# A hybrid encoder layer on one core: where the mixers' copies run, the output projection's priority, and the place of x's last rows

## The chip, the cores and the metric

The kernel runs on one core of one Trainium2 chip. A core has five engines that the text names: TensorE (PE; PEld is its loading of weights), VectorE (DVE), ScalarE (ACT), GpSimd (POOL) and SyncE (SP), which here issues nearly all DMAs. Data lies in SBUF; PE writes its sums to PSUM, from where VectorE or ScalarE has to copy them. The metric is the device time of one execution in microseconds (us), the median of several runs.

## The reference, cut to what matters

One inference step of one encoder layer for two groups of frames: 1024 new ones (`x_prompt`, T rows 0 to 1023) and 64 of running streams (`x_sample`, rows 1024 to 1087), width 1024.

```python
p = _rmsnorm(x, norm_mix[l]) @ w_in[l]            # all mixers' inputs, 3076 columns
conv_o, conv_h = _conv_module(cv_a, cv_g, ...)    # gate, depthwise conv of 31 taps, layer norm over 256, silu
fox_o = ...                                       # softmax attention with forget gates, blocks of 128 rows
s_fin, hg_o = lax.scan(_hgrn_chunk ...)           # gated linear recurrence in chunks of 64
sb_o = ...                                        # stick-breaking attention
mix = concat[conv_o, fox_o, hg, sb_o]             # 4 x 256 columns
x = x + mix @ w_out[l]
x = x + _mem_attend(_rmsnorm(x, norm_mem[l]), mk, mv, w_mq[l], w_mo[l])
h = _rmsnorm(x, norm_ffn[l])
return x + jnp.square(jax.nn.relu(h @ w_up[l])) @ w_down[l]
```

The last step is one more norm. Outputs are both groups' results and the new caches and states.

## The kernel before

Everything is kept transposed, features on the partitions and the 1088 rows along the free axis. A dense product in full precision is made from three: each operand is split into a high and a low part (`split`, the line of VectorE's half is L171, ScalarE's is L74), and `mm3` issues for each of the 8 blocks of the contraction two matmuls with the weights' high part (`wh`) and one with the low part (`wl`). All matmuls are recorded at L71.

The stages, in program order:

- *Start.* SP loads the nine row tiles `xt0` to `xt8` (L254). PE transposes them block by block into `px` (L282), ScalarE and VectorE scale and split `px` (L285) and copy it (`xs`, L289) to `xT_d` in DRAM; `stats` makes the rows' norms and spreads them with `dg` and `pr` over the partitions (`rb`). `xt0` to `xt6` have buffers of their own, `xt7` lies in a buffer of the tag "vn", and `xt8`, which holds `x_sample`, in the only buffer of the tag "kT". The first `kT` of the attention (the stick-breaking lane's keys, L441) therefore waits until PE has transposed all of `xt8`.
- *Mixers.* Four lanes are written as generators: projections, attention (fox and stick-breaking), convolution, HGRN. The loop at the end interleaves their steps by estimated time and gives each a priority (`tc.cur_priority`); a scheduler then lays down a fixed order for each engine, in which of the instructions that can go the one of the smallest number goes first. Projections have the smallest, then attention, HGRN, convolution and the products of the memory (PR_MM); everything that follows has PR_END, the largest. Each engine works through its order strictly; SP's DMAs too.
- *Copies.* Attention transposes its weights on PE (`pt`, L517); `evac` copies them from PSUM to `aT`, and the attention's and HGRN's results likewise (`o`, `hvn`, `hkn`, `hsc`). A counter sends each fourth copy to VectorE (L310), the others to ScalarE.
- *Convolution.* Two tiles of 128 channels (`y_4800` and `y_4816`), three chunks of rows, 31 taps each on VectorE (L794). In the last chunk the new conv cache is copied out (`cvo`, L805). Then, for either half of the chunk, PE sums over channels (`pme`), VectorE subtracts the mean (L816), ScalarE squares, PE sums again (`pva`), and the norm (L149, L152 to L154), scale and bias (L825, L826), sigmoid (ScalarE, L166) and product (L830) follow; SP stores the result to `mix_d`, slots 0 and 1 (L832 to L835). `cv` has a single PSUM buffer.
- *Output projection.* `split_mix` (L1036 and after) loads a slot of `mix_d` and splits it: slots 0 and 1 are the convolution, 2 and 3 fox, 4 and 5 HGRN, 6 and 7 stick-breaking. `dense_add(0, w_out, ...)` adds the product for group 0 (rows 0 to 511), 8 x 8 x 3 = 192 matmuls `pa` of 512 columns, and L1120 adds `pa` to x. The norm for the memory's attention follows, then `dense_add(1, ...)` for group 1 (576 rows, in 320 and 256 columns), whose order MIX takes slots 0 and 1 last. The convolution's last chunk belongs to group 1 alone.
- *After that* memory attention, the MLP up and down, and the final norm; their order is the same in both kernels.

Of the kernel before, what the change touches and what calls it, by code (L numbers as in the profile page):

```python
# [8 lines left out]
F32 = mybir.dt.float32  # L9
# [3 lines left out]
AF = mybir.ActivationFunctionType  # L13
# [4 lines left out]
P = 128  # L18
D = 1024
# [3 lines left out]
T = SP + SS  # L23
# [15 lines left out]
P_COST = 18.0  # L39
PROJ_ORDER = "sb0 h0 sb1 ff cv fox0 h1 fox1 kv".split()  # L40

PR_PROJ, PR_ATT, PR_HGRN, PR_CONV, PR_MM, PR_END = (i * 10 ** 6 for i in (1, 2, 3, 4, 5, 10))


class Need:
# [7 lines left out]
def kernel(ctx: ExitStack, tc: tile.TileContext, *args):  # L53
# [16 lines left out]
    def mm(out, lhsT, rhs, start, stop, **kw):  # L70
        nc.tensor.matmul(out, lhsT=lhsT, rhs=rhs, start=start, stop=stop, **kw)  # L71

    def act(out, in_, func, **kw):
        nc.scalar.activation(out=out, in_=in_, func=func, **kw)  # L74

    V, Q = nc.vector, nc.gpsimd
# [33 lines left out]
    for m in LEVELS[1:]:  # L110
        nb = 64 // m
        f = const.tile([P, nb], F32, name=f"lf{m}", tag="lvlf", bufs=1)
# [27 lines left out]
    def rstd_chain(pool, n, mean_sq, tag, scale=1.0, parts=P, out=None, tiles=None):  # L140

        tags = [tag + c for c in "vyt"] if isinstance(tag, str) else tag
        tags = [dict(tag=g) if isinstance(g, str) else dict(zip(("tag", "bufs"), g)) for g in tags]
        if tiles:
            v, y, t = tiles[0][:, :n], out, tiles[1][:, :n]
        else:
            v, y, t = (out if c == "y" and out is not None else pool.tile([P, n], F32, name="rs" + c, **g)[:parts]
                       for c, g in zip("vyt", tags))
        V.tensor_scalar(out=v, in0=mean_sq, scalar1=scale, scalar2=EPS, op0=ALU.mult, op1=ALU.add)  # L149
        act(y, v, AF.Ln)  # L150
        act(y, y, AF.Exp, scale=-0.5)
        V.tensor_tensor(out=t, in0=y, in1=y, op=ALU.mult)  # L152
        V.scalar_tensor_tensor(out=t, in0=t, scalar=-0.5, in1=v, op0=ALU.mult, op1=ALU.mult)
        V.scalar_tensor_tensor(out=y, in0=t, scalar=1.5, in1=y, op0=ALU.add, op1=ALU.mult)  # L154
        return y
# [21 lines left out]
    def fetch_w(src, r0, kt, c0, cols=P):  # L177
        raw = wp.tile([P, KD, P], F32, name="wr", tag="wr")[:, :kt, :cols]
        nc.sync.dma_start(out=raw, in_=src[r0:r0 + kt * P, c0:c0 + cols].rearrange("(k p) c -> p k c", p=P))
        return raw  # L180
# [60 lines left out]
    att = mx.enter_context(tc.tile_pool(name="att", bufs=2))  # L241
    wk = mx.enter_context(tc.tile_pool(name="wk", bufs=2))
    rb = wk.tile([P, T], F32, name="rb", tag="rb", bufs=1)
    with ExitStack() as pa:
        xa = pa.enter_context(tc.tile_pool(name="xa", bufs=1))
        ps_a = pa.enter_context(tc.tile_pool(name="ps_a", bufs=4, space=PSUM))
        ss = xa.tile([P, 9], F32, name="ss")
        V.memset(ss, 0.0)
        junk = att.tile([P, 2, D], BF16, name="junk", tag="vn")
        xt = []  # L250
        for i, (t0, n) in enumerate(TT):
            xt.append((att.tile([P, T], F32, name=f"xt{i}", tag=("vn", "kT")[i - 7], bufs=(2, 1)[i - 7])[:, :D] if i >= 7 else
                       xa.tile([P, D], F32, name=f"xt{i}")))
            nc.sync.dma_start(out=xt[i][:n], in_=x_prompt[t0:t0 + n] if i < 8 else x_sample)  # L254
            if i in (3, 6):
                c = (C_SK, C_SV)[i // 3 - 1]
                early[c] = fetch_w(w_in, 0, KD, c)

        def stats(c0, cn, tiles):
            for i in tiles:  # L260
                n = TT[i][1]
                if i % 2:
                    V.tensor_tensor_reduce(out=junk[:n, 1], in0=xt[i][:n], in1=xt[i][:n], scale=1.0, scalar=0.0,
                                           op0=ALU.mult, op1=ALU.add, accum_out=ss[:n, i:i + 1])
                else:
                    act(junk[:n, 0], xt[i][:n], AF.Square, accum_out=ss[:n, i:i + 1])
            r = rstd_chain(xa, len(tiles), ss[:, tiles[0]:tiles[0] + len(tiles)], "ra", scale=1.0 / D)
            pr = ps_a.tile([P, 512], F32, name="pr", tag="pr", bufs=1)
            for j, i in enumerate(tiles):
                n = TT[i][1]  # L270
                dg = xa.tile([P, P], F32, name="dg", tag="dg", bufs=2)
                V.tensor_scalar(out=dg[:n, :n], in0=ident[:n, :n], scalar1=r[:n, j:j + 1], scalar2=None, op0=ALU.mult)
                mm(pr[:, j * P:j * P + n], ones[:n], dg[:n, :n], True, True)
            act(rb[:, c0:c0 + cn], pr[:, :cn], AF.Copy)

        for c0, cn in CH:
            tiles = [i for i, (t0, n) in enumerate(TT) if c0 <= t0 < c0 + cn]
            for k in range(KD):
                px = ps_a.tile([P, 512], F32, name="px", tag="px")
                for i in tiles:  # L280
                    t0, n = TT[i]
                    nc.tensor.transpose(px[:, t0 - c0:t0 - c0 + n], xt[i][:n, k * P:(k + 1) * P], ident[:n, :n])  # L282
                hi, lo = h_at(k, c0, cn)
                act(hi, px[:, :cn], AF.Identity, scale=g_mix[:, k:k + 1])
                V.scalar_tensor_tensor(out=lo, in0=px[:, :cn], scalar=g_mix[:, k:k + 1], in1=hi.bitcast(F32),  # L285
                                       op0=ALU.mult, op1=ALU.subtract)
                xs = xa.tile([P, 512], F32, name="xs", tag="xs", bufs=4)
                if k % 2:
                    V.tensor_copy(out=xs[:, :cn], in_=px[:, :cn])  # L289
                else:  # L290
                    act(xs[:, :cn], px[:, :cn], AF.Copy)
                nc.sync.dma_start(out=xT_d[:, k, c0:c0 + cn], in_=xs[:, :cn])
            stats(c0, cn, tiles)
# [6 lines left out]
    ps_cv = mx.enter_context(tc.tile_pool(name="ps_cv", bufs=1, space=PSUM))  # L300
    hc = mx.enter_context(tc.tile_pool(name="hc", bufs=1))

    flip = [0]

    def evac(out, in_):
        flip[0] = (flip[0] + 1) % 4
        if flip[0]:
            act(out, in_, AF.Copy)
        else:
            V.tensor_copy(out=out, in_=in_)  # L310

    pending = [None, 0]

# [702 lines left out]
    while lanes:  # L1016
# [13 lines left out]
            ln.need = y.key  # L1030
        else:
            ln.t += y * ln.rate
    tc.cur_priority = PR_END

    def split_mix(k, src, t0, n, which):
        nc.sync.dma_start(out=src, in_=mix_d[k][:, t0:t0 + n])  # L1036
# [28 lines left out]
    def wide():  # L1065
        return unit("aq")
# [11 lines left out]
    def rms_stats(g, psum, tag, tiles=None, keep=False, s2=None):  # L1078

        if not s2:  # L1080
            for k in range(KD):
                s2 = add_square(g, k, s2, wide())
        rr = unit("tm")
        for c0, cn in GR[g][2]:
            ps = psum.tile([P, 512], F32, name="pr", tag=tag)
            mm(ps[:, :cn], ones, s2[:, c0:c0 + cn], True, True)
            v, t = tiles or (unit("tm"), unit("tm"))
            rstd_chain(None, cn, ps[:, :cn], "xxx", scale=1.0 / D, out=rr[:, c0:c0 + cn], tiles=(v, t))
            if keep:
                V.tensor_tensor(out=t[:, :cn], in0=v[:, :cn], in1=rr[:, c0:c0 + cn], op=ALU.mult)  # L1090
                nc.sync.dma_start(out=rms_d[:, c0:c0 + cn], in_=t[:, :cn])
        return rr
# [7 lines left out]
    def rms_apply(g, gains, rr, which, over=False):  # L1100

        dst = [pair(which) for _ in range(KD)]
        for c0, cn in GR[g][2]:
            for k in range(KD):
                hf = normed(g, k, gains, rr, c0, cn, xT[g][k] if over else None)
                split(dst[k][0][:, c0:c0 + cn], dst[k][1][:, c0:c0 + cn], hf[:, :cn])
        return dst

    def dense_add(g, src, r0, kt, a, psum, ahead=None, store=False, after=None, order=None):

        t0, n, _ = GR[g]
        for m in (0, 4, 1, 5, 2, 6, 3, 7) if after else range(KD):
            w = load_w(src, r0, kt, m * P)
            if ahead:
                ahead(m)
            for c0, cn in GR[g][2]:
                ps = psum.tile([P, 512], F32, name="pa", tag="mm")
                mm3(ps[:, :cn], w, lambda k: (a[k][0][:, c0:c0 + cn], a[k][1][:, c0:c0 + cn]), kt, order=order)
                xs = xT[g][m][:, c0:c0 + cn]
                V.tensor_tensor(out=xs, in0=xs, in1=ps[:, :cn], op=ALU.add)  # L1120
            if store:
                nc.sync.dma_start(out=x2_d[m][:, t0:t0 + n], in_=xT[g][m])
            if after:
                tc.cur_priority += 600
                after(m)
                tc.cur_priority -= 600
# [3 lines left out]
    with ExitStack() as pm_:  # L1130
# [94 lines left out]

        MIX = (2, 3, 4, 5, 6, 7, 0, 1)
        dense_add(0, w_out, 0, KD, mix[0], ps1, ahead)
        h2 = rms_apply(0, g_mem, rms_stats(0, ps2, "sc"), 0)
        dense_add(1, w_out, 0, KD, mix[1], ps1, lambda m: load_x(1, m), order=MIX)
        for g in range(2):  # L1230
# [321 lines left out]
```

## Time and profile before

| | us |
|---|---|
| median of 3 runs | 1765.38 (1765.11 to 1768.04) |
| the profiled execution | 1760.05 |
| its span, first to last instruction | 1758.3 |
| PE busy | 1694.8 (96%) |
| VectorE busy | 1172.1 (67%) |
| ScalarE busy | 791.4 (45%) |
| mean granted clock of PE | 0.991 |

The profile is one execution, recorded by the hardware profiler; times count from the first instruction. "Busy" leaves out the issuing of DMAs, and PE's matmuls are pipelined, so that their rows overlap. An idle time is put down to the instruction that released it, the one that came last. The granted clock is PE's, as a share of its full 2.4 GHz: 0.50 is its lower level of 1.2 GHz, and a window between the two has parts at either.

### The profile page before, as it was taken

The page shows a single profiled execution, that of the slowest core. Times are in us where ns is not written, and L with a number is a line of the kernel's source. Part 1 is how long each engine was busy: PE and PEld are TensorE (multiplying, and loading weights), DVE is VectorE, ACT ScalarE, POOL GpSimd, SP SyncE. Part 2 cuts the span into 40 slices and gives each one's busy share as a digit, 9 for nine tenths or more (in the row PEclk, how much of TensorE's full clock was granted, in tenths as well). Part 3 has the DMA queues.
Part 4 walks back from the last instruction along what each step waited for, and adds up shares of the span by engine and source line. Part 5 has one row for each costly group of instructions (what it writes and reads, how often), then busy time and mean ns, then how long its engine had stood idle before and what let it go on. Part 6 is the DMA issues. An engine that isn't in the chain of part 4 may idle for free.

```text
span 1758.3 us, 29395 instructions
## 1 busy us (share of the span) xinstructions
PE 1694.8 (96%) x11379; PEld 1504.8 (86%) x11379; DVE 1172.1 (67%) x2231; ACT 791.4 (45%) x1614; POOL 94.1 (5%) x201
## 2 busy tenths in 40 slices
PE   6999999999989979999999999999999999999997
PEld 4987768787777768988899989999999999999987
DVE  6266789988986897667777696555556444444435
ACT  6265657547447855346456363433334212122213
POOL 3021111101120200000000000000000000000000
PEclk9999999999999989999999999999999999999999
DMA  8521332242237348232522343333335722332112
GB/s 256 142 80 33 111 87 88 71 123 76 71 95 215 111 140 254 73 97 67 156 78 73 101 124 99 99 106 99 101 105 203 266 94 87 99 100 74 37 37 102
DMA packets 233195, 194.70 MB, mean 111 GB/s; under 512 B 17502, under 2 KB 199711, under 8 KB 233055
## 3 DMA queue, kind: packets, MB, share of 16 engines
q1 hardware_dynamic: 232639, 192.54, 35.6%
q8 instruction: 90, 1.47, 0.4%
q14 instruction: 50, 0.41, 0.1%
q10 hardware_dynamic: 160, 0.26, 0.0%
q0 software_dynamic: 256, 0.01, 0.0%
HBM read 137.96 MB, written 53.72 MB: 109 GB/s over the span
## 4 chain that ended last, share of the span: by engine, by line
PE 75%; DVE 15%; ACT 4%; DMA 3%; issue 2%; POOL 0%; SPq 0%; DVEq 0%; POOLq 0%; ACTq 0%
PE pz L71 24%; PE pw L71 15%; PE pm L71 11%; PE pa L71 9%; PE pq L71 5%; PE z L71 2%; DVE y L794 2%; PE pmo L71 2%; PE pms L71 1%; PE po L71 1%; PE pt L517 1%; PE pv L71 1%; DVE wl L171 1%; DVE hsc L934 1%; DVE sba L494 1%
## 5 line engine op out<-in xcount | busy, mean ns | idle before, releaser
L74 ACT ACTIVATE wh<-wr 128x1024 fp32r<-128x1024 f32 (+1 forms) x179 | 161.4, 909 | 439.6 <-PE pz L71 195.2
L171 DVE TENSOR_TENSOR wl<-wr,wh 128x1024 fp32r<-128x1024 f32 (+1 forms) x179 | 184.3, 1036 | 63.8 <-ACT wh L74 62.5
L71 PE MATMUL pw<-ap,wh 128*128 128x512 f32 x720 | 223.3, 391 | 1.0 <-DVE xt L1120 0.6
L71 PE MATMUL pz<-ap,wh 128*128 128x288 f32 x988 | 198.3, 294 | 0.0
L71 PE MATMUL pa<-ap,wh 128*128 128x256 f32 (+2 forms) x768 | 187.0, 332 | 2.1 <-DVE xt L1120 2.1
L71 PE MATMUL pm<-hx,wh 128*128 128x512 f32 (+1 forms) x640 | 176.6, 363 | 2.1 <-ACT wh L74 1.4
L71 PEld LDWEIGHTS pz<-ap,wh 128*128 128x128 f32 x988 | 161.3, 188 | 4.6
L71 PE MATMUL pm<-ap,wh 128*128 128x256 f32 (+1 forms) x768 | 164.7, 307 | 0.0
L71 PEld LDWEIGHTS pw<-ap,wh 128*128 128x128 f32 x720 | 130.0, 188 | 23.5 <-issue 0.8
L71 PE MATMUL pz<-ap,wl 128*128 128x288 f32 x494 | 145.4, 294 | 0.0
L71 PEld LDWEIGHTS pa<-ap,wh 128*128 128x128 f32 x768 | 132.3, 191 | 12.5 <-DVE xt L1120 2.4
L71 PE MATMUL pw<-ap,wl 128*128 128x512 f32 x360 | 140.3, 390 | 0.0
L71 PEld LDWEIGHTS pm<-hx,wh 128*128 128x128 f32 x640 | 110.2, 192 | 20.6 <-ACT wh L74 2.2
L71 PEld LDWEIGHTS pm<-ap,wh 128*128 128x128 f32 x768 | 123.8, 191 | 4.2 <-issue 1.7
L71 PE MATMUL pa<-ap,wl 128*128 128x512 f32 (+2 forms) x384 | 127.2, 332 | 0.1
L1349 DVE TENSOR_TENSOR xt<-xt,pz 128x576 f32<-128x576 f32 x56 | 42.2, 753 | 115.6 <-PE pz L71 108.8
L71 PE MATMUL pm<-ap,wl 128*128 128x256 f32 (+1 forms) x384 | 114.0, 297 | 0.0
L71 PE MATMUL pm<-hx,wl 128*128 128x512 f32 (+1 forms) x320 | 112.7, 352 | 0.1
L794 DVE SCALAR_TENSOR_TENSOR y<-ext,cwT,y 128x376 f32<-128x376 f32 (+1 forms) x180 | 100.9, 604 | 0.3
L1349 DVE TENSOR_TENSOR xt<-xt,pw 128x512 f32<-128x512 f32 (+2 forms) x80 | 51.0, 638 | 69.8 <-PE pw L71 67.6
L71 PE MATMUL pq<-ap,wh 128*128 128x512 f32 (+2 forms) x384 | 93.0, 331 | 0.0
L71 PEld LDWEIGHTS pz<-ap,wl 128*128 128x128 f32 x494 | 92.7, 188 | 0.0
(385 smaller groups left out, 3572.9 us busy)
## 6 DMA issues: line engine op xcount, KB each, us to landing
wr<-in_w_up_dram SPq DMA_DIRECT2D x32, 512.0 KB, 4.1
wr<-in_w_down_dram SPq DMA_DIRECT2D x32, 512.0 KB, 3.5
wr<-in_w_in_dram SPq DMA_DIRECT2D x24, 512.0 KB, 4.3
hid_d<-ap SPq DMA_DIRECT2D x32, 288.0 KB, 2.4
aq<-hid_d SPq DMA_DIRECT2D x32, 288.0 KB, 3.7
wr<-in_w_out_dram SPq DMA_DIRECT2D x16, 512.0 KB, 4.2
wr<-in_w_mq_dram SPq DMA_DIRECT2D x16, 512.0 KB, 3.8
wr<-in_w_mo_dram SPq DMA_DIRECT2D x32, 256.0 KB, 2.8
```

Source lines behind the costliest of these rows:

```text
L71: nc.tensor.matmul(out, lhsT=lhsT, rhs=rhs, start=start, stop=stop, **kw)
L74: nc.scalar.activation(out=out, in_=in_, func=func, **kw)
L171: V.tensor_tensor(out=lo, in0=src, in1=hi.bitcast(F32), op=ALU.subtract)
L494: V.tensor_tensor_scan(out=v[:, ::-1], data0=z[:, n - 1:0:-1], data1=v[:, ::-1], initial=-NEG, op0=ALU.add, op1=ALU.subtract)
L517: nc.tensor.transpose(ps[:w, j - jb], p[:, j * P:j * P + w], ident)
L794: V.scalar_tensor_tensor(out=y, in0=ext[:, j:j + n], scalar=cwT[:, ct, j:j + 1], in1=y, op0=ALU.mult, op1=ALU.add)
L934: V.copy_predicated(sc[r, s_at:s_at + ng, :, r].rearrange("p g h (c w) -> p (g h) c w", w=2 * m)[:, :, :, m:], lvl[m][r, par * nb:(par + 1 ...
L1349: eng.tensor_tensor(out=out, in0=a, in1=b, op=ALU.add)
```

## The change

Three edits. First, `evac` always uses ScalarE; the counter goes. 40 copies move: 11 of `aT` with 512 columns, 4 with 384, 6 with 256 and 4 with 128, 7 of `o`, and 8 of HGRN's and others. Second, a priority PR_OUT lies between HGRN and the convolution, whose number and that of the memory's products rise by one; the splits of `mix` and group 0 of the output projection get it, and what follows has PR_END as before. Third, `xt8` lies in the buffer of the tag "q2" and no longer in that of "kT". Lines after `evac` move up by five.

```diff
--- before.py
+++ after.py
@@ -39,7 +39,7 @@
 P_COST = 18.0
 PROJ_ORDER = "sb0 h0 sb1 ff cv fox0 h1 fox1 kv".split()
 
-PR_PROJ, PR_ATT, PR_HGRN, PR_CONV, PR_MM, PR_END = (i * 10 ** 6 for i in (1, 2, 3, 4, 5, 10))
+PR_PROJ, PR_ATT, PR_HGRN, PR_OUT, PR_CONV, PR_MM, PR_END = (i * 10 ** 6 for i in (1, 2, 3, 4, 5, 6, 10))
 
 
 class Need:
@@ -249,8 +249,9 @@
         junk = att.tile([P, 2, D], BF16, name="junk", tag="vn")
         xt = []
         for i, (t0, n) in enumerate(TT):
-            xt.append((att.tile([P, T], F32, name=f"xt{i}", tag=("vn", "kT")[i - 7], bufs=(2, 1)[i - 7])[:, :D] if i >= 7 else
-                       xa.tile([P, D], F32, name=f"xt{i}")))
+            xt.append(att.tile([P, T], F32, name="xt7", tag="vn")[:, :D] if i == 7 else
+                      att.tile([P, 2, T], F32, name="xt8", tag="q2", bufs=1)[:, 0, :D] if i == 8 else
+                      xa.tile([P, D], F32, name=f"xt{i}"))
             nc.sync.dma_start(out=xt[i][:n], in_=x_prompt[t0:t0 + n] if i < 8 else x_sample)
             if i in (3, 6):
                 c = (C_SK, C_SV)[i // 3 - 1]
@@ -300,14 +301,8 @@
     ps_cv = mx.enter_context(tc.tile_pool(name="ps_cv", bufs=1, space=PSUM))
     hc = mx.enter_context(tc.tile_pool(name="hc", bufs=1))
 
-    flip = [0]
-
     def evac(out, in_):
-        flip[0] = (flip[0] + 1) % 4
-        if flip[0]:
-            act(out, in_, AF.Copy)
-        else:
-            V.tensor_copy(out=out, in_=in_)
+        act(out, in_, AF.Copy)
 
     pending = [None, 0]
 
@@ -1030,7 +1025,7 @@
             ln.need = y.key
         else:
             ln.t += y * ln.rate
-    tc.cur_priority = PR_END
+    tc.cur_priority = PR_OUT
 
     def split_mix(k, src, t0, n, which):
         nc.sync.dma_start(out=src, in_=mix_d[k][:, t0:t0 + n])
@@ -1225,6 +1220,7 @@
 
         MIX = (2, 3, 4, 5, 6, 7, 0, 1)
         dense_add(0, w_out, 0, KD, mix[0], ps1, ahead)
+        tc.cur_priority = PR_END
         h2 = rms_apply(0, g_mem, rms_stats(0, ps2, "sc"), 0)
         dense_add(1, w_out, 0, KD, mix[1], ps1, lambda m: load_x(1, m), order=MIX)
         for g in range(2):
```

The three fences below show each engine's fixed order, so `x4` are four instructions in a row.

PE at the start, before: `px` are the transposes of x (`xt_240` holds `x_sample`), `pr` spreads the norms, `pn` transposes the first keys, `pm` are projection matmuls.

```order
L282 MATMUL px<-ident,xt_234 128x128
L282 MATMUL px<-ident,xt_238 128x128
L282 MATMUL px<-ident,xt_240 128x64
L71 MATMUL pr<-dg,ones 128x128
L71 MATMUL pr<-dg,ones 128x64
L482 MATMUL pc<-ident,kv 128x128
L365 MATMUL pn<-ident,kT 128x128 x4
L482 MATMUL pc<-ident,kv 128x128 x3
L71 MATMUL pm<-ap,wh 128x256 x2
```

The same place after:

```order
L283 MATMUL px<-ident,xt_238 128x128
L283 MATMUL px<-ident,xt_240 128x64
L360 MATMUL pn<-ident,kT 128x128 x4
L71 MATMUL pm<-ap,wh 128x256 x2
L71 MATMUL pm<-ap,wl 128x256
L71 MATMUL pm<-ap,wh 128x256 x2
L71 MATMUL pm<-ap,wl 128x256
L71 MATMUL pm<-ap,wh 128x256 x2
L71 MATMUL pm<-ap,wl 128x256
L71 MATMUL pm<-ap,wh 128x256 x2
L71 MATMUL pm<-ap,wl 128x256
L71 MATMUL pr<-dg,ones 128x128 x2
```

The keys' transposes and twelve projection matmuls have moved ahead of the last transposes of x.

PE where the mixers end, before: `pv` is the last attention, `pa` the output projection, `pme` and `pva` the convolution's two sums.

```order
L71 MATMUL pv<-aT,vn 64x128 x5
L71 MATMUL pa<-ap,wh 128x512 x4
L71 MATMUL pme<-y_4800,ones 128x183
L71 MATMUL pme<-y_4816,ones 128x183
L71 MATMUL pa<-ap,wl 128x512
L71 MATMUL pa<-ap,wh 128x512 x2
L71 MATMUL pa<-ap,wl 128x512
L71 MATMUL pva<-sq_5331,ones 128x183
L71 MATMUL pva<-sq_5332,ones 128x183
```

PE after, at the end of group 0:

```order
L71 MATMUL pa<-ap,wh 128x512 x2
L71 MATMUL pa<-ap,wl 128x512
L71 MATMUL pva<-sq_5332,ones 128x183
L71 MATMUL pa<-ap,wh 128x320 x2
L71 MATMUL pa<-ap,wl 128x320
```

The other sums stand among earlier matmuls `pm`; the last `pva` has moved behind all 192 `pa` of group 0.

VectorE at the end of the taps, before (the taps L794 of either tile stand 23 in a row ahead of this):

```order
L794 SCALAR_TENSOR_TENSOR y_4800<-ext_4785,cwT,y_4800 128x366
L794 SCALAR_TENSOR_TENSOR y_4816<-ext_4801,cwT,y_4816 128x366
L805 COPY cvo<-pco 30x256 x2
L171 TENSOR_TENSOR ap<-mix,ap 128x512
L171 TENSOR_TENSOR wl<-wr,wh 128x1024
L816 SCALAR_TENSOR_TENSOR y_4800<-pme,y_4800 128x183
```

The same end of the taps after:

```order
L171 TENSOR_TENSOR ap<-mix,ap 128x512
L789 SCALAR_TENSOR_TENSOR y_4800<-ext_4785,cwT,y_4800 128x366
L171 TENSOR_TENSOR ap<-mix,ap 128x512
L966 TENSOR_TENSOR ho<-htv,po 128x64
L789 SCALAR_TENSOR_TENSOR y_4816<-ext_4801,cwT,y_4816 128x366
L171 TENSOR_TENSOR wl<-wr,wh 128x1024
L789 SCALAR_TENSOR_TENSOR y_4800<-ext_4785,cwT,y_4800 128x366
```

The splits of `mix` and of the weights have moved in among the taps.

## Rows read from the trace of the kernel before

**Rows 1.** Busy line of the page: busy us, share of span, instructions

```profile
PE 1694.8 (96%) x11379; PEld 1504.8 (86%) x11379; DVE 1172.1 (67%) x2231; ACT 791.4 (45%) x1614; POOL 94.1 (5%) x201
```

**Rows 2.** What PE waits for: us in total, times, longest us

```profile
PE pme L71 <- DVE cvo L805: 9.1, 1, 9.1
...
PE z L71 <- DVE sba L494: 3.2, 4, 1.1
...
PE pt L517 <- ACT sba L74: 2.6, 6, 0.8
...
PE pd L71 <- DVE hsc L934: 2.5, 2, 2.0
...
PE pv L71 <- ACT aT L74: 1.4, 2, 0.9
```

**Rows 3.** Window: length, busy PE PEld DVE ACT POOL, PEclk, DMA share, GB/s

```profile
308.00:352.00 44.00, 41.99 (x319) 33.75 (x319) 41.61 (x75) 26.18 (x45) 6.38 (x11) 1.00 0.27 72
```

**Rows 4.** Window, line L310 alone: length, VectorE busy, then as above

```profile
0.00:720.00 720.00, 18.55 (x40) 0.98 0.42 121
```

**Rows 5.** Groups by form: busy us, mean ns, idle before, releaser

```profile
L310 DVE COPY aT<-pt 128x512 f32<-128x512 f32 x11 | 7.5, 683 | 0.2 <-PE pt L517 0.2
...
L74 ACT ACTIVATE aT<-pt 128x512 f32<-128x512 f32 x41 | 24.3, 593 | 17.6 <-PE pt L517 17.4
```

**Rows 6.** Timeline, VectorE, start: start us, us, instruction, idle before, releaser

```profile
43.89 0.67 DVE L441 TENSOR_TENSOR kT<-pm,rb 128x512 f32<-128x512 f32 x1
```

**Rows 7.** Timeline, PE, start of the kernel

```profile
40.69 1.21 PE L282 MATMUL px<-ident,xt 128*128 128x128 f32 x6 [0.95 <-ACT xs L74]
...
43.47 1.41 PE L71 MATMUL pr<-dg,ones 128*128 128x128 f32 x4 [1.57 <-DVE dg L272]
```

**Rows 8.** Windows at the start

```profile
44.00:48.00 4.00, 3.47 (x16) 3.09 (x15) 1.33 (x4) 2.08 (x4) 2.19 (x5) 0.50 0.41 121
48.00:52.00 4.00, 4.00 (x29) 3.87 (x28) 0.80 (x2) 0.67 (x2) 0.84 (x1) 0.76 0.40 113
```

**Rows 9.** Timeline, VectorE, end of the mixers

```profile
641.37 11.82 DVE L794 SCALAR_TENSOR_TENSOR y<-ext,cwT,y 128x366 f32<-128x366 f32 x23
...
653.78 0.67 DVE L171 TENSOR_TENSOR ap<-mix,ap 128x512 fp32r<-128x512 f32 x1
```

**Rows 10.** Timeline, PE, end of the mixers and group 0 of the output projection

```profile
643.60 1.20 PE L71 MATMUL pa<-ap,wh 128*128 128x512 f32 x4
653.90 1.59 PE L71 MATMUL pme<-y,ones 128*128 128x183 f32 x4 [9.11 <-DVE cvo L805]
...
661.29 0.78 PE L71 MATMUL pva<-sq,ones 128*128 128x183 f32 x4
661.78 0.52 PE L71 MATMUL pa<-ap,wl 128*128 128x512 f32 x1
...
701.26 0.45 PE L71 MATMUL pa<-ap,wh 128*128 128x320 f32 x2
```

**Rows 11.** Window right after the long wait

```profile
652.00:656.00 4.00, 1.95 (x5) 1.48 (x6) 4.00 (x9) 0.09 (x1) 0.00 (x0) 0.50 0.08 24
```

**Rows 12.** Windows, tile pa alone: busy PE, PEld, VectorE, then as above

```profile
676.00:700.00 24.00, 24.00 (x108) 19.87 (x107) 2.73 (x4) 1.00 0.75 230
708.83:715.23 6.40, 6.40 (x50) 6.40 (x49) 0.41 (x1) 1.00 0.03 10
```

**Rows 13.** Timeline, the last convolution step: VectorE, then SyncE, then ScalarE

```profile
662.89 0.34 DVE L149 TENSOR_SCALAR rs<-pva 128x183 f32<-128x183 f32 x1
...
669.72 0.60 DVE L825 TENSOR_TENSOR y<-y,sq 128x183 f32<-128x183 f32 x2
...
673.73 0.60 DVE L830 TENSOR_TENSOR y<-y,sq 128x183 f32<-128x183 f32 x2
...
676.97 0.79 SPq L1036 DMA_DIRECT2D aq<-mix_d  x2
...
680.64 0.67 ACT L74 ACTIVATE ap<-aq 128x576 fp32r<-128x576 f32 x1
```

## Prediction

> **What bounds the kernel now.** The first view to read is the busy line of the page: TensorE (PE) is busy 96% of 1758.3 us, VectorE (DVE) 67%, ScalarE (ACT) 45% [rows 1]. So the end is set by PE, and a change of copies between the two other engines can pay only where PE stands still, or where PE runs at the lower clock after standing still. The second view is the list of what PE waits for. Its longest single wait is 9.1 us at the end of the mixers, for VectorE; the others that name VectorE or ScalarE in the mixers are 1.4 to 3.2 us each, in pieces of about 1 us or less but for one of 2.0 [rows 2]. The third is windows of the mixers' long middle: in 308 to 352 us PE is busy 41.99 of 44 us, VectorE 41.61, ScalarE 26.18 [rows 3]. There VectorE is as full as PE, and ScalarE has 17.8 us to spare. The fourth is the timeline at the two ends of the mixers, where PE's order is changed.
>
> The sum is made on the profiled execution: 1760.05 us, of which 1758.3 are the span. The median of the three runs is 1765.38, that is 5.33 more; I carry the difference over unchanged, so the same saving is taken off the median.
>
> **Part one: the copies.** The 40 copies that VectorE makes at L310 take 18.55 us of it in all [rows 4]. A copy of the widest form takes 683 ns on VectorE and 593 on ScalarE [rows 5], a ratio of 0.868, so ScalarE gets about 18.55 x 0.868 = 16.1 us. I cost neither at its face. On ScalarE's side the cover is its idle time: 16.1 us spread over some 550 us of mixers, beside 17.8 us idle in 44 alone [rows 3]. On VectorE's side the order of the changed program shows that the freed time is filled at once with convolution taps that used to stand later; between two steps on which attention depends, VectorE has about the same amount of work as before. Queued behind an added copy on ScalarE stand the next exponentials and squares of the lanes, and PE waits for those through pt and pv. The bounds: if the added copies make the waits that name ScalarE (2.6 and 1.4) twice as long, +4.0; if the lighter VectorE removes those that name it (3.2 and 2.5), -5.7 [rows 2]. I take 0, midway as near as rows can tell, and keep -6 to +4.
>
> One rule speaks against this part. In the trace the two engines share these copies 1 to 3, and VectorE is the fuller one [rows 3]. The Trainium skill, "TensorEngine Tiling (Array Packing)", section "PSUM Bottleneck", says to use both ScalarE and VectorE to empty PSUM, since the copying can become the bottleneck. By that rule the sum would take on up to the whole of the added ScalarE time; by the row it takes on nothing, because the engine given the copies is the emptier. No run here yet shows all of them on ScalarE.
>
> **Part two: the rows of x_sample (xt8).** They no longer sit in the buffer of kT. Before, the first kT of the stick-breaking attention is written at 43.89 [rows 6], only after PE has transposed xt8, and with it the projection behind it is held back. PE has nothing but the tail of the transposes, and idles 0.95 and 1.57 us in front of them [rows 7]. The granted clock is 0.50 in 44 to 48 and 0.76 in 48 to 52 [rows 8], so half a step of 4 us and a quarter of another are lost: (1 - 0.50) x 4 + (1 - 0.76) x 4 = 3.0. In the changed order four transposes of kT and twelve projection matmuls (and more after the next pair of pr) stand between the same transposes: work that is ready fills the gaps. Removed at most: 2.5 of idle time and 3.0 of clock, 5.5; I take 5, because a fill that runs a little late leaves a gap. The bounds are -8 (other short gaps in front of 40 us go too, the largest are of the kind just named) and 0 (the first projection groups wait for weight or norm steps on VectorE at that place, and nothing is filled). The DMA of xt8 itself stays in its place on SP's queue; only the address changes, and its cost is nothing: q2's buffer is first needed later.
>
> **Part three: the end of the mixers.** Before, PE starts the output projection with four pa at 643.60 and then waits 9.11 us, to 653.90, for the convolution's means (pme). VectorE meanwhile runs 23 taps in a row for 11.82 us and only then the copies L805 and the split of mix at 653.78, which the next pa needs [rows 9, 10]. After that wait the clock is 0.50 through 656 [rows 11]. Group 0 of the projection (192 pa of 512 columns) ends at 701.26 [rows 10], 57.66 us after its start. In 676 to 700, 108 of these pa take 24.00 us [rows 12], so 192 take 192 x 24.00 / 108 = 42.7 undisturbed. Four bundles of statistics lie between them, each about 0.5 of PE's own time (pva at 661.29, the next pa at 661.78) [rows 10]: 2.0. So 57.66 - 42.7 - 2.0 = 13.0 us are lost here: 9.1 of wait, about 3.9 of lower clock and of short hand-overs.
>
> In the changed order the splits of mix stand between the taps, group 0 runs as 192 pa on end, and three of the four statistics bundles stand among earlier projection matmuls. There the third waits for VectorE's subtraction and ScalarE's square; no row of before shows that short wait alone, it lies between nothing and a step like 1.57 [rows 7], and I take 1.5. But the last pva (second half, conv slot 1) now stands behind all 192 pa, because the convolution's priority is lower than that of the output projection. What hangs on it: first four norm steps of 0.34 [rows 13], an x update of about 0.7 in front and one weight split of 1.2 between, about 3.2 us; then the scale, bias, sigmoid and product, 669.72 to 673.73 + 0.60 in before, 4.6; then the store to mix_d and the load back, issued at 676.97, 2.6 later; the split by ScalarE at 680.64, 3.7 later, and 0.67 for it and the like for the low part [rows 13]. That is 3.2 + 4.6 + 2.6 + 3.7 + 0.7 = 14.8, 14 to 15.5. PE has cover for it: 54 pa of group 1 on the other six slots, at 6.40 / 50 = 0.128 each [rows 12], 6.9 us. The rest, some 7.5 us, is a **moved wait** that did not exist before, and a lower clock behind it, by half of the 3.9 found above about 2. Together 9.5. Queued behind it on SP are the reads of the memory's keys and values and the next weights; PE's own group 1 is what waits.
>
> Net of part three: -13.0 + 1.5 + 9.5 = -2.0, and since 13.0 holds hand-overs that stay (about 0.3), -1.7. Bounds: -7 (the chain without weight splits between, 10 us, so a 3 us gap) and +4 (the chain stretched on VectorE as before, where the same steps from the first at 662.89 to 674.33 take 11.4 us [rows 13] in place of 7.8, and the third bundle waiting longer).
>
> **Sum.** 0 - 5 - 1.7 = -6.7. Profiled 1760.05 - 6.7 = 1753.35; median 1765.38 - 6.7 = 1758.7.
>
> **Rivals.** First, *no change*: the start's fill fails, because VectorE's rms and split steps pace the first projections (VectorE's kT step stands between idle pieces of PE there). Then only -1.7 is left, 1763.7. For it: PE's idle pieces at 40 to 45 name VectorE and ScalarE [rows 7]. Against: twelve matmuls whose input is split already stand ready in the order.
>
> Second, *more*: the moved wait shrinks to 3 us, since fewer weight splits stand between the chain's steps in the order than before, and most of the middle's waits for VectorE go: -5 - 7 - 4.4 of the 5.7 = -16.4, 1749. For it: only a short list of steps stands between that pva and the store in the changed order. Against: two trips through the DMA and both engines stay in the chain.
>
> Third, *slower*: ScalarE paces PE in the middle. Its place is the attention stretch (100 to 620 us), its price the whole 16.1 us of added copies, since each pt must be emptied before the next can be written: -6.7 + 16.1 = +9.4, 1774.8. It decides from the point at which more than (6.7 + 3.5) / 16.1, 63%, of the added time lies on PE's path. For it: pt already waits for ScalarE at six places [rows 2]. Against: 17.8 idle us of 44 on ScalarE [rows 3]. The rule of the Trainium skill quoted above would end in this rival.
>
> Fourth, *it doesn't do what it says*: the order shows that every copy is on ScalarE and that group 0 is unbroken, so there is no chance left for that.
>
> **How the numbers follow.** Forecast 0.60, no change 0.20, more 0.12, slower 0.08. About 0.2%, 3.5 us, is what a measurement of this kernel can tell from no change; forecast and *more* lie beyond it, 0.72 faster, 0.20 within, 0.08 slower. The range: the parts' bounds added with their signs are far apart, -21 and +8, but need not fall together; The range lets *more* in to its full -16.4, lets *no change* in with the third part at +4 and 1.4 still gained at the start (+2.6), and leaves *slower* out: 1749 to 1768, all but about 0.2 of the chance, since each case may also miss its own value.
>
> **What would show it.** Right: PE at 40 to 47 us shows pn and pm between px and no gap over 0.5 us, with a clock above 0.5 in 44 to 48; no pme wait near 640; group 0 takes 43 to 44 us; and a new PE wait of some 7 us, pa for ScalarE's ap, shortly behind the end of group 0. Wrong: a half-clock stretch that stays at 44 us (part two), a wait of 12 us or none at the split of slot 0 (part three), or waits of pt and pv for ScalarE that together pass 10 us (part one, the third rival). The stages from the memory attention on keep their order, so a difference there of over 1 us would be one that I have not accounted for.

## The result and the profile after

The changed kernel takes 1755.34 us (median of 4 runs, 1753.96 to 1755.46) where the kernel before took 1766.14 beside it: a ratio of 0.9936, 95% interval 0.9919 to 0.9953. A second measurement gave 1755.31 against 1763.06, 0.9955 (0.9942 to 0.9969). So it is faster by 0.45 to 0.64%, 8 to 11 us; forecast were 6.7. The profiled execution took 1755.36 us, its span is 1753.6, 4.7 less than that of before.

The change in the sums is small. PE's busy line after, against [rows 1]: VectorE has 13.8 us less, ScalarE 13.5 more, and PE's share is what it was.

```profile
PE 1690.9 (96%) x11366; PEld 1501.5 (86%) x11379; DVE 1158.3 (66%) x2191; ACT 804.9 (46%) x1654; POOL 99.1 (6%) x201
```

What PE waits for after, against [rows 2] (us in total, times, longest): `pme` has gone from the list, and a wait of `pa` for ScalarE's split stands in its place. In the middle the wait of `z` for `sba` has grown from 3.2 to 4.6, one of `pt` for ScalarE's `aT` is new (before, PE waited 1.4 for such a copy at `pv`, and 1.2 for one by VectorE at `pt`), and `pd` has shrunk from 2.5 to 0.4.

```profile
PE pa L71 <- ACT ap L74: 4.9, 1, 4.9
PE z L71 <- DVE sba L489: 4.6, 8, 0.7
...
PE pt L512 <- ACT aT L74: 3.6, 6, 1.6
PE pt L512 <- ACT sba L74: 2.5, 7, 0.6
...
PE pd L71 <- DVE hsc L929: 0.4, 1, 0.4
```

The start, PE's timeline and then the two windows that answer to [rows 8]: the first keys and the projection stand between the transposes, and the granted clock is full, where it was 0.50 and 0.76.

```profile
35.49 2.30 PE L283 MATMUL px<-ident,xt 128*128 128x128 f32 x12
37.72 0.66 PE L360 MATMUL pn<-ident,kT 128*128 128x128 f32 x4
38.13 0.48 PE L71 MATMUL pm<-ap,wh 128*128 128x256 f32 x2
```

```profile
44.00:48.00 4.00, 4.00 (x36) 4.00 (x35) 2.38 (x9) 0.80 (x2) 0.00 (x0) 1.00 0.80 244
48.00:52.00 4.00, 4.00 (x28) 3.50 (x26) 0.34 (x3) 1.19 (x3) 2.34 (x5) 1.00 0.30 89
```

The end of the mixers, PE's timeline, against [rows 10]: group 0 starts at 647.46 and ends at 691.30, 43.84 us in place of 57.66. Then 54 `pa` of group 1, and the moved wait.

```profile
647.46 0.73 PE L71 MATMUL pa<-ap,wh 128*128 128x512 f32 x2 [0.47 <-ACT mnat L74]
...
691.12 0.47 PE L71 MATMUL pva<-sq,ones 128*128 128x183 f32 x2
691.30 0.58 PE L71 MATMUL pa<-ap,wh 128*128 128x320 f32 x2
...
703.90 1.43 PE L71 MATMUL pa<-ap,wh 128*128 128x320 f32 x4 [4.87 <-ACT ap L74]
```

The chain behind that wait, against [rows 13], on VectorE, SyncE and ScalarE: 7.15 us from the last `pva` at 691.12 to the end of the product at 698.27, the load back issued 1.75 later, the split 3.1 after that.

```profile
691.92 0.34 DVE L149 TENSOR_SCALAR rs<-pva 128x183 f32<-128x183 f32 x1
...
697.65 0.62 DVE L825 TENSOR_TENSOR y<-y,sq 128x183 f32<-128x183 f32 x2 [0.16 <-ACT sq L74]
```

```profile
700.02 1.27 SPq L1031 DMA_DIRECT2D aq<-mix_d  x2
```

```profile
703.16 0.68 ACT L74 ACTIVATE ap<-aq 128x576 fp32r<-128x576 f32 x1 [3.21 <-DMA aq<-mix_d]
```

The windows right behind it show what the lower clock adds: 0.50 in 704 to 708 is (1 - 0.50) x 4 = 2.0 us, so the moved wait costs 4.9 + 2.0, about 7.

```profile
700.00:704.00 4.00, 0.10 (x1) 0.10 (x1) 1.26 (x3) 0.84 (x2) 0.00 (x0) 0.68 0.70 208
704.00:708.00 4.00, 4.00 (x15) 3.67 (x16) 3.68 (x7) 3.63 (x8) 0.00 (x0) 0.50 0.25 84
```

### The profile page after: what moved, and what is told of

Its sections match the earlier page's. It is cut to its first block, busy times and chain, and to the rows that moved or that the text cites. A ratio compares the mean times of both kernels' runs of the same rounds, so it can differ in the third digit from the quotient of the medians.

```text
span 1753.6 us, 29391 instructions
## 1 busy us (share of the span) xinstructions
PE 1690.9 (96%) x11366; PEld 1501.5 (86%) x11379; DVE 1158.3 (66%) x2191; ACT 804.9 (46%) x1654; POOL 99.1 (6%) x201
## 4 chain that ended last, share of the span: by engine, by line
PE 75%; DVE 12%; ACT 5%; DMA 4%; issue 3%; POOL 1%; SPq 0%; DVEq 0%; POOLq 0%; ACTq 0%
PE pz L71 24%; PE pw L71 16%; PE pm L71 11%; PE pa L71 9%; PE pq L71 4%; PE z L71 2%; DVE sba L489 2%; PE pt L512 2%; PE pmo L71 2%; PE pms L71 1%; PE pv L71 1%; PE po L71 1%; ACT sba L74 1%; DVE wl L171 1%; DVE y L789 1%
```

## The experiments

Each kernel was timed against the kernel before on the same chip. The first question is which of the three parts gives the gain.

**Copies alone** (the kernel before, with this edit only):

```diff
     def evac(out, in_):
-        flip[0] = (flip[0] + 1) % 4
-        if flip[0]:
-            act(out, in_, AF.Copy)
-        else:
-            V.tensor_copy(out=out, in_=in_)
+        act(out, in_, AF.Copy)
```

> The kernel before with the copies of evac all on ScalarE, nothing else. First theory (as predicted): nothing is gained or lost in the middle, ratio to before 0.999 to 1.001. Second theory (read from the trace of after, where the 20th load of projection weights stands 6.4 us later than in before although the start had gained 5.3): the copies cost PE about 5 us, ratio 1.003. Third: the lighter VectorE brings the convolution forward, and part of the 9.1 us wait for pme goes with it, ratio 0.997 or less.

Measured 1756.20 against 1763.86 us, ratio 0.9955 (0.9942 to 0.9967): the third theory. The wait for `pme` is gone without any change of priority. VectorE's timeline of before and of this kernel, then PE's of this one: the copies `cvo`, which end the taps, stand at 627.25 (653.11 before), and the last `pva` ahead of group 0.

```profile
653.11 0.74 DVE L805 COPY cvo<-pco 30x256 f32<-30x256 f32 x2
```

```profile
627.25 0.41 DVE L799 COPY cvo<-pco 30x256 f32<-30x256 f32 x1
```

```profile
644.29 0.79 PE L71 MATMUL pva<-sq,ones 128*128 128x183 f32 x4
...
650.00 0.73 PE L71 MATMUL pa<-ap,wh 128*128 128x512 f32 x2 [0.78 <-ACT mnat L74]
```

**xt8 alone** (the kernel before with the third edit only: `tag="q2"` in place of "kT" for `xt8`).

> The kernel before with x_sample's rows in the buffer of the tag q2, nothing else. First theory: 36 to 48 us is filled and its half clock goes, 5 us, ratio 0.997. Second theory: what is won at 48 us is lost again in the mixers, where VectorE (busy 41.6 of 44 us) sets the pace, ratio 0.999 to 1.001, with the wait of pme at the end longer than 9.1 us.

Measured 1756.93, ratio 0.9970 (0.9957 to 0.9982), 5.3 us: the first theory. The wait for `pme` is 9.1 us as before, so nothing is lost in the mixers that was won at the start. Its windows:

```profile
44.00:48.00 4.00, 4.00 (x36) 4.00 (x35) 2.62 (x10) 1.26 (x4) 0.00 (x0) 1.00 0.75 245
48.00:52.00 4.00, 4.00 (x29) 3.74 (x28) 0.58 (x4) 0.76 (x2) 1.48 (x4) 1.00 0.38 80
```

**Priority alone** (the kernel before with PR_OUT, as in the change).

```diff
-    tc.cur_priority = PR_END
+    tc.cur_priority = PR_OUT
...
         dense_add(0, w_out, 0, KD, mix[0], ps1, ahead)
+        tc.cur_priority = PR_END
```

> The kernel before with the output projection's own priority, nothing else. First theory (as predicted): the wait for pme and its low clock, 13 us, go, and the moved wait takes 9 to 10 of it back; net 2 us, ratio 0.999. Second theory (read from after, where the moved wait measures 4.9 us): net 5 to 9 us, ratio 0.995 to 0.997. Third: without the moved copies VectorE is too full to have the splits of mix ready, PE waits for them within group 0, ratio 1.000 or more.

Measured 1761.57, ratio 0.9982 (0.9972 to 0.9991), 3.2 us, between the first two theories and nearer to the first. Its moved wait, from the list of PE's waits, is 8.8 us and not 4.9:

```profile
PE pa L71 <- ACT ap L74: 8.8, 1, 8.8
```

VectorE's timeline tells why: 11 taps still stand in a row at 643.96, when the copies are still on it, so that all the statistics of the last chunk fall behind group 0, and not only the last `pva`.

```profile
643.96 5.69 DVE L794 SCALAR_TENSOR_TENSOR y<-ext,cwT,y 128x366 f32<-128x366 f32 x11
```

**The conv's tail ahead of the projection** (the kernel after, with one line).

```diff
             if last:
+                tc.cur_priority = PR_HGRN + 500000
                 ps = ps_cv.tile([P, 2, G], F32, name="pco", tag="cv")
```

> The kernel after, with the statistics and the tail of the convolution's last chunk at a smaller number than the output projection, so that all four pva stand ahead of group 0. First theory: the wait of 4.9 us for ScalarE's ap and its low clock go, and the time is 4 to 6 us below after's 1755, ratio to before 0.990 to 0.992. Second theory: pva's wait for VectorE and ScalarE then stands in front of group 0 instead, and PE loses there what it wins behind it, ratio as after's, 0.993 to 0.995.

Measured 1751.16, ratio 0.9936 (0.9919 to 0.9952): inside the second theory's range, and not told apart from after (0.9936 and 0.9955) by time. The trace is of an execution at the slow end of this kernel's (1755.40, where its runs go from 1749.16 to 1757.08). In it the wait of `pa` for `ap` has gone, as the first theory has it, but most of its 7 us is lost again: the clock is 0.57 in 648 to 652, at the first matmuls of group 0 (1.00 in after), and up to 713.47 `pa` waits 2.1 us for VectorE's update of x (0.8 in after), with 0.66 around it. PE comes to the memory attention at 749.84, only 2.0 before after. Those 2.0 too are lost by the end, in part between 1000 and 1020, where the clock is 0.91 (1.00 in after).

```profile
648.00:652.00 4.00, 3.59 (x9) 2.87 (x10) 2.91 (x8) 1.84 (x8) 0.00 (x0) 0.57 0.77 221
712.00:716.00 4.00, 2.53 (x12) 2.54 (x13) 4.00 (x8) 1.31 (x2) 0.00 (x0) 0.66 0.00 0
1000.00:1020.00 20.00, 18.20 (x108) 16.57 (x107) 18.10 (x30) 10.29 (x18) 0.00 (x0) 0.91 0.62 187
```

The second question is how the parts stand to one another, measured together on one chip.

**After without the copies** (xt8 and priority; `flip` is put back into after).

> The kernel after with every fourth copy back on VectorE: priority and xt8 together. First theory (the freed VectorE time, not the priority, removes the wait for pme): the two parts add up as they measured alone, 0.9982 and 0.9970, ratio 0.995, and the moved wait of pa for ScalarE's ap is again about 9 us where after has 4.9. Second theory (priority and copies need each other little): ratio as after's, 0.9936.

**After without the priority** (copies and xt8; the second edit is undone).

> The kernel after without the output projection's own priority: copies and xt8 together. First theory: the copies alone make the taps end some 25 us earlier, all four statistics come ahead of group 0, and the priority then only adds the moved wait; the parts add up, 0.9955 and 0.9970, ratio 0.9925, below after's 0.9936. Second theory: the priority still gives 3 us beside them, and this kernel is slower than after, ratio 0.995 or more.

**After, unchanged.**

> The kernel after, unchanged, on the same chip as the others of this call. Both theories: 0.9936 of before, within 0.9919 to 0.9953.

| kernel | us | ratio to before (1763.06) | span of the profile |
|---|---|---|---|
| xt8 and priority | 1755.85 | 0.9953 (0.9938 to 0.9969) | 1753.6 |
| copies and xt8 | 1749.27 | 0.9923 (0.9909 to 0.9936) | 1750.6 |
| all three (after) | 1755.31 | 0.9955 (0.9942 to 0.9969) | 1753.8 |

The first theory holds for the first two kernels. After, unchanged, came out above the range that was expected of it, though the two intervals overlap. Two pairs of parts add: 0.9982 x 0.9970 = 0.9952, and 0.9955 x 0.9970 = 0.9925. Copies and priority do not: beside the priority (and xt8) the copies give nothing (0.9955 against 0.9953), and beside the copies the priority costs 0.3% (0.9955 against 0.9923, intervals apart). PE's timeline of the first kernel has group 0 start 5.9 us earlier than in after (647.46), and the moved wait, 8.7 us here, end where it ends in after (703.90):

```profile
641.54 0.73 PE L71 MATMUL pa<-ap,wh 128*128 128x512 f32 x2
...
704.16 1.43 PE L71 MATMUL pa<-ap,wh 128*128 128x320 f32 x4 [8.70 <-ACT ap L74]
```

**Copies and xt8 again**, on another chip:

> Copies and xt8 without the priority, the same program as before under that name, beside the others of this call. 0.9923, within 0.9909 to 0.9936, if the advantage over after is one of the program and not of the chip.

1751.33 against 1764.58, ratio 0.9926 (0.9913 to 0.9938). The version that beats both kernels is the change without its second part.

The third question is what makes the taps end earlier.

**Fewer taps** (the kernel before, `for j in range(CW - 5)` in the convolution).

> The kernel before with 26 of the convolution's 31 taps (the last five are left out, so the convolution computes something else): 30 instructions of about 0.6 us, 18 us, are taken from VectorE, and every copy stays where it was. First theory (what counts is how much VectorE has to do before the taps end): the wait of 9.1 us for pme goes as it went with the copies, ratio 0.994 to 0.997. Second theory (the copies that attention waits for are what counts): the taps' end moves by no more than the 10 taps of the last chunk, 6 us, a wait of about 3 us stays, ratio 0.998.

Measured 1753.04 (0.9944, 0.9930 to 0.9957), the first theory: with every copy where it was, the wait for `pme` is gone, and `cvo` stands at 622.84.

```profile
622.84 0.73 DVE L805 COPY cvo<-pco 30x256 f32<-30x256 f32 x2
```

**Every second copy on VectorE** (the other way).

```diff
-        flip[0] = (flip[0] + 1) % 4
+        flip[0] = (flip[0] + 1) % 2
```

> The kernel before with the copies turned the other way: every second one on VectorE in place of every fourth, some 18 us more for it and 16 less for ScalarE. First theory (VectorE's load before the end of the taps sets the wait for pme): the taps end about 15 to 25 us later against PE, the wait grows from 9 to 20 us or more, ratio 1.006 to 1.015. Second theory (sharing the copies between both engines helps attention): ratio below 1.

Measured 1758.70 against 1764.58, ratio 0.9967 (0.9955 to 0.9980): faster, against the first theory. The window of line L310 alone has 81 copies, 38.16 us. More taps are left for the end, 29 in a row and not 23, and the wait has grown from 9.1 to 13.1 us (expected were 20):

```profile
0.00:720.00 720.00, 38.16 (x81) 0.98 0.42 121
```

```profile
637.60 14.89 DVE L794 SCALAR_TENSOR_TENSOR y<-ext,cwT,y 128x366 f32<-128x366 f32 x29
652.40 0.74 DVE L805 COPY cvo<-pco 30x256 f32<-30x256 f32 x2
```

```profile
638.56 1.55 PE L71 MATMUL pa<-ap,wh 128*128 128x512 f32 x4 [0.47 <-ACT mnat L74]
...
653.19 1.59 PE L71 MATMUL pme<-y,ones 128*128 128x183 f32 x4 [13.09 <-DVE cvo L805]
```

But the taps do not end later: `cvo` stands at 652.40, 0.7 ahead of before. The wait has grown because PE comes to the first `pa` at 638.56, 5.0 us earlier than before (9.6 earlier than in before's second profile, below), with the same 3758 matmuls ahead of it in either order. The windows 60 to 620 of three kernels, with no copy, a quarter and half of them on VectorE (copies only, before, this one), show PE busy for 531.66, 534.72 and 536.33 of 560 us:

```profile
60.00:620.00 560.00, 531.66 (x4008) 439.09 (x4020) 446.62 (x910) 347.46 (x791) 77.73 (x132) 1.00 0.35 100
```

```profile
60.00:620.00 560.00, 534.72 (x4053) 442.74 (x4053) 445.32 (x916) 333.32 (x753) 74.62 (x132) 1.00 0.36 100
```

```profile
60.00:620.00 560.00, 536.33 (x4096) 446.50 (x4108) 459.21 (x953) 325.06 (x722) 76.51 (x132) 1.00 0.36 102
```

So in the attention stretch PE idles less where the copies are shared, by 4.7 us between the ends. The idle time explains only 1.6 of the 5.0 us; the start gives some 0.6 and the clock between 520 and 560 us some 1.8, and about 1 us stays without a name. Over the profiles of all kernels here that keep the 31 taps, PE idles 27.0 to 29.3 us of this window with no copy on VectorE (seven profiles) and 24.5 to 27.2 with a quarter (five); half has this one alone, at 23.7. Together they bear out that PE loses time here without copies on VectorE, and the end of the mixers gains; the sizes are not shown, and for half the sign in this window rests on one profile.

**The priority for the splits of mix alone** (the kernel after; `tc.cur_priority = PR_END` already ahead of `dense_add(0, ...)`).

> The kernel after with the output projection's own priority for the splits of mix alone; group 0's matmuls come behind the convolution again. First theory (the moved wait is all that the priority costs): all four pva stand ahead of group 0, ratio as without the priority, 0.992 to 0.993. Second theory: early splits push taps back on VectorE and the statistics later, ratio 0.994 to 0.9955.

Measured 1757.90, ratio 0.9959 (0.9946 to 0.9973): the second theory's number, for a reason that neither had. The statistics do stand ahead of group 0, but PE waits 4.6 us within it for a weight:

```profile
PE pa L71 <- ACT wh L74: 4.6, 1, 4.6
```

ScalarE's timeline has that weight waiting for its DMA, and SyncE issued no weight of the projection between 643.35 and 658.97: eight loads `aq` for group 1 stood ahead on its queue, three of them behind the convolution's last stores. That the queue held the weight back is read from this order, not tried. SyncE, then ScalarE:

```profile
643.35 0.38 SPq L179 DMA_DIRECT2D wr<-in_w_out_dram  x1
...
656.19 2.26 SPq L1031 DMA_DIRECT2D aq<-mix_d  x3
...
658.97 0.42 SPq L179 DMA_DIRECT2D wr<-in_w_out_dram  x1
```

```profile
665.27 1.06 ACT L74 ACTIVATE wh<-wr 128x1024 fp32r<-128x1024 f32 x1 [0.28 <-DMA wr<-in_w_out_dram]
```

**Before, a second profile.**

> The kernel before, unchanged, for a second profile of it on this chip. All theories: ratio 0.999 to 1.001, the wait of pme for cvo again 9 us. If the profile of before shown first was a quick execution only, the span here is 3 to 6 us longer, and the list of PE's waits or the granted clock shows where.

Ratio 0.9997 (0.9986 to 1.0008), runs from 1760.01 to 1768.40. The span is 1762.6, 4.3 more than in the profile shown first, with the same wait of 9.1 for `pme`. PE is at the first `pa` at 648.14 and not 643.60, so the 4.5 us lie ahead of it, in several pieces: PE's busy time in 60 to 620 us is 1.9 less, and the granted clock shows 0.91 in 220 to 240 (1.00 in the first profile) and 0.83 in 540 to 560 (0.96 there, with 0.95 in 520 to 540). The profile shown first was at the quick end of what this kernel does.

## Why the prediction was right, point by point

**The sum** said -6.7 us from the parts 0, -5 and -1.7. The two comparisons of after with before gave 8 and 11; the profiled executions differ by 1760.05 - 1755.36 = 4.7, and by 9.6 where the second profile of before (1764.96) is taken. The prediction carried the 5.33 us between the profiled execution and the median over to after unchanged. That was wrong: after's profiled run lies at its median, and the 5.33 was the place of one quick execution within a spread of 1759.7 to 1768.4.

**xt8: right in mechanism and size.** Forecast 5, alone 5.3 us by the ratio 0.9970. The pieces are those named: PE no longer idles in front of the last transposes, and the clock of 0.50 and 0.76 is 1.00. The rival *no change* falls with it. Of the rival *more*, the moved wait came part of the way (4.9, where it had 3), but the two waits for VectorE in the middle did not go: 5.0 is left of 5.7.

**The end of the mixers: right as a sum, the terms off by up to 3 us.** Group 0 was to take 43 to 44 us, it took 43.84. The moved wait was to be some 7.5 us (14.8 less 6.9 is 7.9) behind 54 `pa`, for ScalarE's `ap`: it came there, at 4.9 us in after, and at 8.8 with the priority alone. Its chain took 703.90 - 691.12 = 12.8 us for the 14.8 put together: up to the product 7.15 for 7.8, the store and load 1.75 for 2.6, the DMA 3.1 for 3.7; and the 54 `pa` that cover it took 7.7 for 6.9. The lower clock cost the 2 that were taken. The priority alone gave 3.2 us, forecast 1.7. But in this change the 13.0 that were put down to it are not its work, since the copies end the wait for `pme` without it (with them alone group 0 takes 43.65, 650.00 to 693.65); what it adds beside them is the moved wait.

**The copies: the value held by luck.** Beside the priority they give nothing, as forecast. But 0 is a balance, and of sizes that the prediction did not have. They make the moved wait 8.7 - 4.9 = 3.8 us shorter than in the kernel without them, because PE comes to group 0 later (647.46 and not 641.54), by the statistics that now stand ahead of it and by more idle time in attention (29.3 us of 60 to 620 in place of 26.1); behind the wait both go on at the same time, 703.90 and 704.16. That the freed time would be filled with taps was right: in 60 to 620 VectorE is busy 445.32 us before and 446.62 with the copies alone. The step that failed is the conclusion drawn from it, that the lighter VectorE is worth nothing outside the two waits of 3.2 and 2.5. The taps that moved forward end at 627.25 and not at 653.11, and with that goes the longest wait, of `pme` for `cvo`, whose end the prediction put down to the priority alone. Copies alone are worth 7.9 us, the largest of the three parts; leaving out 18 us of taps ends the wait as well. Two edits that removed the same wait did not add, and the one with the dearer side effect should go.

The Trainium skill, "TensorEngine Tiling (Array Packing)", section "PSUM Bottleneck", was quoted for a rule against this part: use both engines to empty PSUM, which the section says of a TensorE that tiling has made faster. In the attention stretch the traces agree with it, 28.3, 25.3 and 23.7 us of PE idle with none, a quarter and half of the copies on VectorE. For the whole kernel none (0.9955) and half (0.9967) are not told apart, and both beat the quarter, since with none the wait at the end of the mixers goes. The rival *slower* that went with it needed 63% of 16.1 us on PE's path; the waits that name ScalarE's `aT` grew from 1.4 to 3.9 us.

## What to carry to other kernels

When two edits attack one wait, cost each alone and then both together: here the copies with the priority gave less than the copies without it (0.9955 and 0.9923, both with xt8). A long wait for an engine can be a debt of the whole stretch ahead of it, even where that engine is not full (VectorE was busy 445 of 560 us): work taken from it upstream, copies in one trial and taps in another, ended the wait. A priority that moves work up moves something down, so look in the new order for the last item that was passed, and for the chain that hangs on it.

## What was not expected

The same program's runs spread over 8 us (1760.01 to 1768.40 for before), and one profile may sit at an edge, so the difference of two profiled executions can be off by as much (4.7 or 9.6 here). Medians of several runs give the size, and profiles show where it comes from. And moving copies either way from the quarter that was there made the kernel faster, 0.9955 with none on VectorE and 0.9967 with half: the quarter seems to sit between two stretches that want opposite things. Whether half of the copies in attention with a lighter VectorE at the end would gain on both sides was not tried.
